# Ninth seven-product couple in the down-projections of a two-layer encoder trunk, with its weight differences formed on the fly

## The chip, the cores and the metric

The kernel runs on one core of one Trainium2 chip. The metric is the device time of one launch in microseconds (us), taken as the median of several runs. Each profile is of one execution.

The engines are called as the profile calls them: PE (TensorE; PEld is its weight load), DVE (VectorE), ACT (ScalarE), POOL (GpSimd) and SP (SyncE, which here issues nearly all DMAs).

## The reference

The trunk has two layers, 256 tokens, a model width of 2048 and an inner width of 5504, all in float32. Each layer is RMSNorm, token mixer, residual add, RMSNorm, ConvGLU, residual add. Layer 0's mixer is a bidirectional mLSTM, layer 1's a bidirectional HGRN2. The change concerns the last product of the ConvGLU, `@ w_down`:

```python
def conv_glu(hn, w_up, conv_w, conv_b, w_down):
    u = hn @ w_up
    a, v = jnp.split(u, 2, axis=-1)
    ...
    for j in range(CONV_W):
        c = c + ap[:, j:j + s] * conv_w[j]
    return (jax.nn.gelu(c, approximate=False) * v) @ w_down

    ...
    for layer in range(DEPTH):
        ...
        h = h + mix
        h = h + conv_glu(rmsnorm(h, norm_ffn_g[layer]), ...)
    return rmsnorm(h, final_g)
```

## The kernel before

**Split products.** Each float32 operand is held as a high and a low part (`wh`, `wl` for weights), and a product is three matmuls: high by high, high by low, low by high. ACT makes `wh` from a loaded weight block by a cast (line 146), DVE makes `wl` by a subtraction (line 147). Such a pair of tiles, 128x1024 or 128x512, is called a piece. Pieces are fetched three ahead of their use, and there are four `wh`/`wl` buffers, with two more in the output stages for every third piece.

**Stages.** Everything is one stream of chunks: layer 0's mixer projections and its output product, the 43 up-projection chunks (called "fm" in the code) in two halves of 22 and 21, and after each half a down-projection of that half's 22 or 21 row blocks of `w_down`. Layer 1 has the same, with its own mixer.

**Down-projection and couples.** A down-projection runs as two pairs of column blocks, one after the other: output columns 0 to 1023, then 1024 to 2047. Within a pair, two row blocks of weights make a couple, numbered `u` from 0. An ordinary couple takes eight 128x512 products, 24 matmuls. A couple listed in `SEVEN` uses Strassen's scheme of seven products, 21 matmuls; it needs sums of the activations (`sx`, made once for each half by `token_sums`, lines 546 to 551) and differences of the weight blocks (T1 to T4).

**Where the weight differences come from.** In the ConvGLU they are all formed earlier: `prepare` (line 611) loads a couple's weights while other stages run, forms the differences on DVE and stores them to DRAM (`tscr`). The down-projection then loads 1536 columns of the weights, 512 of the differences into the same `raw` tile and 1536 into a `T` tile. The mLSTM's output product does it otherwise: its three seven-product couples have nothing stored, and `combine` (lines 201 to 207) forms the differences from the couple's 2048 loaded columns by four DVE subtractions just before they are split ("on the fly").

**End of the seven-product part.** After the last listed couple of a pair, `mid` (lines 563 to 571) adds the four accumulators P1, P5, P6, P7 to the residual `hm`: one ACT copy, six DVE operations and two POOL additions. `done` (line 577) adds the other four at the pair's end. At the end of layer 0's second half the next norm's transposes (line 423) and its `xt` operands (lines 368 and 369) for the first eight row blocks are made between `mid` and the pair's end.

**Order.** A scheduler orders each engine's instructions at build time. The weight loads marked `late` keep their program order on SP's queue.

**Constants.** One tile `cst` of 928 columns, kept for the whole program, holds the identity (128 columns), two masks and a summing matrix of the mLSTM (640) and level masks of the HGRN2 (160).

The lists before are `SEVEN = (2, 3, 4, 5, 6, 7, 8, 9), (1, 2, 3, 4, 5, 6, 7)` for the first and second half, for both layers alike.

Of the kernel before, what the change touches and what calls it, by code (L numbers as in the profile page):

```python
# [8 lines left out]
F32 = mybir.dt.float32  # L9
F32R = mybir.dt.float32r  # L10
I32 = mybir.dt.int32
# [4 lines left out]
P = 128  # L16
# [30 lines left out]
LEAD = 48  # L47
TEMP = 3
GATES = 4 * AH
SEVEN = (2, 3, 4, 5, 6, 7, 8, 9), (1, 2, 3, 4, 5, 6, 7)  # L50
FIRST = 6
SPLIT = (0, 2, 5), (0, 2, 5)
END = 3
# [5 lines left out]
LEVELS = (1, 2, 4, 8, 16, 32, 64)  # L59
FINE = 5  # L60
C_ID, C_MF, C_MB, C_SUM, C_LV = 0, 128, 384, 640, 768
NCST = C_LV + FINE * QUAD


def trunk_kernel(ctx, tc, xT, x_d, fg_d, pp_d, cst_d, w_gate, w_first, w_aq, w_ak, w_av, w_ao, w_aout, w_ao2,
# [8 lines left out]
    psa = ctx.enter_context(tc.tile_pool(name="psa", bufs=4, space=PSUM))  # L74

    pp = keep.tile([P, NPP], F32, name="pp")
    cst = keep.tile([P, NCST], F32, name="cst")
    ones = keep.tile([P, T], F32, name="ones")
    pad = keep.tile([P, 8], F32, name="pad")
    hmx = keep.tile([P, 2], F32, name="mhalf")  # L80
    hm = keep.tile([P, 2, D], F32, name="hm")
    ident = cst[:, C_ID:C_ID + P]

    def col(name, i):
        o = OFF[name] + i
# [297 lines left out]
    def late(dst, src):  # L383
        tc.keep_in_program_order(nc.sync.dma_start(dst, src))
# [283 lines left out]
    def mlstm(norm, nxt):  # L668
        YT = [None] * KT
        H = 64  # L670
        stack, startup = ExitStack(), ExitStack()
        sp = startup.enter_context(tc.tile_pool(name="sp", bufs=1))
        gx = sp.tile([P, KT + KT * T], F32, name="gx")
        wg = sp.tile([P, KT * GATES], F32, name="wg")
# [4 lines left out]
        def load(loaded, follower):  # L679

            raws = [keep.tile([P, 512], F32, tag=f"yt{k}", name=f"raw{k}") for k in range(KT)]

            def w(k):
                pin(nc.sync.dma_start(raws[k], w_first[:, k * 512:(k + 1) * 512]))

            def x(q, a, b):
                q.dma_start(gx[:, a:b], xT[:, a:b])

            x(nc.scalar, 0, KT + T)
            x(nc.scalar, KT + T, KT + 2 * T)  # L690
# [12 lines left out]
            for c in range(2):  # L703
                for t in range(2):
                    late(hm[:, t, c * 1024:(c + 1) * 1024], x_d[t, :, c * 1024:(c + 1) * 1024])
            late(cst[:, 0:C_LV], cst_d[:, 0:C_LV])
            late(pp, pp_d)
            return raws

# [15 lines left out]
        def gates(gs):  # L725
            with tc.tile_pool(name="gt", bufs=1) as gp:
                R = norm.R
                gz = gp.tile([P, T], F32, name="gz")
                pg = aux("pg")
                pe.matmul(pg[:, 0:T], cst[:, C_SUM:C_SUM + P], gs, start=True, stop=True)  # L730
                dve.tensor_tensor(gz, pg[:, 0:T], R, ALU.mult)
                dve.tensor_scalar(gz, gz, col("b_gate", 0), None, ALU.add)
                xf = gp.tile([H, T], F32, tag="xf", name="xf")
                e = gp.tile([H, T], F32, name="e")
                u = gp.tile([H, T], F32, tag="u", name="u")
                l = gp.tile([H, T], F32, tag="l", name="l")
                lf = gp.tile([H, T], F32, name="lf")
                dve.tensor_scalar(xf, gz[H:P], 0.0, None, ALU.min)
                act.activation(e, gz[H:P], AF.Abs)
                act.activation(e, e, AF.Exp, scale=-1.0)  # L740
                dve.tensor_scalar(u, e, 1.0, None, ALU.add)
                act.activation(l, u, AF.Ln)
# [33 lines left out]
        segs = [  # L776
            (0, 256, 0, 0, 0, cst[:, C_MF:C_MF + 256]),
            (256, 384, 1, 0, 128, cst[:, C_MF:C_MF + 128]),
            (384, 512, 0, 1, 0, cst[:, C_MB + 128:C_MB + 256]),
            (512, 768, 1, 1, 0, cst[:, C_MB:C_MB + 256]),  # L780
        ]

        def two_parts(ps, name, scale=None):
# [162 lines left out]
    def hgrn(norm, nxt):  # L946
# [3 lines left out]

        def begin():
            mp = box["mp"] = stack.enter_context(tc.tile_pool(name="hg", bufs=1))
            late(cst[:, C_LV:], cst_d[:, C_LV:])
            prepare_early(mp, 1, 30.0, 38.0)
            box["turn"] = 0
            lb = box["lb"] = mp.tile([P, KT], F32, name="lb")
# [49 lines left out]
        def head(hd):  # L1006
# [28 lines left out]
            def both(ps):  # L1035
                return ps.rearrange("p (a b) -> p a b", a=2)

            step = SPREAD if hd < BH - 2 else STEP
            mask = [cst[:, C_LV + i * QUAD:C_LV + (i + 1) * QUAD].bitcast(I32).unsqueeze(1).broadcast_to([P, 2, QUAD])
                    for i in range(FINE)]  # L1040
            ms, n = [gather(1)], T
            yield step
# [107 lines left out]
    def ffn(layer, norm, nxt):  # L1150
# [40 lines left out]
        for part, (f0, nf) in enumerate(((0, FA), (FA, FB))):  # L1191
# [8 lines left out]
                                  todo, 18.0, (nf * 10.4 - 26.0) / len(todo), finished, late, True))  # L1200

            for i in range(nf):
                chunks.append(Chunk("fm", w_up[layer, f0 + i], KT, norm.x, done_up(f0 + i, i, GT, SX, SEVEN[part]),
                                    prep if i == 0 else None,
                                    swap=(2,) if part and i == 0 else (3,) if f0 + i == 1 else (), paced=True))
            def two(src, c0, norm, seven, shares, GT=GT, SX=SX, nf=nf):
                ch = pair(src, nf, c0, lambda k: GT[k], lambda u: SX[u], norm, seven)
                ch.waits, left = [], list(seven)
                for n, (todo, finished) in zip(shares, [early[layer]] + lists):
                    for u in left[:n]:  # L1210
                        store(ch, src, u, todo)
# [5 lines left out]
                return ch  # L1217

            w0, w1 = w_d0[layer][:, f0 * 1024:(f0 + nf) * 1024], w_d3[layer] if part else w_d1[layer]
            n = len(SEVEN[part])  # L1220
            chunks.append(two(w0, 0, nxt if part else None, SEVEN[part], (0, 0, n) if part else (FIRST, n - FIRST)))
            chunks.append(two(w1, 2, nxt if part and not ending else None, SEVEN[part], SPLIT[layer] if part else (0, n)))
            if part:
                chunks[-1].last = ending
                if ending:
# [106 lines left out]
def build(nc, ins, out_shape=(2, P, D), **kw):  # L1332
# [1 line left out]
          for k, a in ins.items()}  # L1334
    out = nc.dram_tensor("out", out_shape, F32, kind="ExternalOutput").ap()
    mscr = nc.dram_tensor("mscr", (64, T), F32, kind="Internal").ap()
    tscr = nc.dram_tensor("tscr", (len(SEVEN_MIX) + 4 * len(SEVEN[0]) + 4 * len(SEVEN[1]), P, 2048), F32, kind="Internal").ap()
    with tile.TileContext(nc, schedule_with_timeline_sim=True) as tc:  # L1338
        with ExitStack() as ctx:
            trunk_kernel(ctx, tc, ap["xT"], ap["x"], ap["fg"], ap["pp"], ap["cst"], ap["w_gate"], ap["w_first"],  # L1340
# [15 lines left out]
```

## Time and profile before

| | us |
|---|---|
| median of 3 runs | 2373.69 (2372.8 to 2375.37) |
| the profiled execution | 2372.06 |
| its span, first to last instruction | 2370.1 |
| PE busy | 2357.5 (99%) |
| DVE busy | 1965.9 (83%) |
| ACT busy | 1464.1 (62%) |
| POOL busy | 196.9 (8%) |

The granted TensorE clock is 0.999 over the span. In the profile's rows a matmul's duration is longer than its distance to the next one, since matmuls are pipelined; so the busy time of PE says that it never waits long, and what a matmul costs is read from the distance between starts. A row of the groups reads: line, engine, operation, output and inputs, shapes and count, then busy us and mean ns of one, then the idle time before them and what ended it. A row of the timeline reads: start and duration in us, engine, line, operation, names, count, and in brackets the idle time before it.

The stages that the change touches lie, in us from the span's start, at 635 to 744 (layer 0, first half), 977 to 1084 (layer 0, second half) and 1914 to 2024 (layer 1, first half). Layer 1's second half, 2256 to 2361, keeps its couples.

### The profile page before, as it was taken

The page shows a single profiled execution, that of the slowest core. Times are in us where ns is not written, and L with a number is a line of the kernel's source. Part 1 is how long each engine was busy: PE and PEld are TensorE (multiplying, and loading weights), DVE is VectorE, ACT ScalarE, POOL GpSimd, SP SyncE. Part 2 cuts the span into 40 slices and gives each one's busy share as a digit, 9 for nine tenths or more (in the row PEclk, how much of TensorE's full clock was granted, in tenths as well). Part 3 has the DMA queues.
Part 4 walks back from the last instruction along what each step waited for, and adds up shares of the span by engine and source line. Part 5 has one row for each costly group of instructions (what it writes and reads, how often), then busy time and mean ns, then how long its engine had stood idle before and what let it go on. Part 6 is the DMA issues. An engine that isn't in the chain of part 4 may idle for free. (4 is left out here: it accounts for less than half of the span.)

```text
span 2370.1 us, 38326 instructions
## 1 busy us (share of the span) xinstructions
PE 2357.5 (99%) x14548; PEld 2019.1 (85%) x14548; DVE 1965.9 (83%) x3028; ACT 1464.1 (62%) x2321; POOL 196.9 (8%) x244
## 2 busy tenths in 40 slices
PE   9999999999999999999999999999999999999998
PEld 8888888888888888888888888888888888888886
DVE  7777687888888898887887888778789888888988
ACT  7655456555565555675777777776555566555565
POOL 0100000000000000000232322220000000000000
PEclk9999999999999999999999999999999999999999
DMA  8776656888988888986666666646788898888896
GB/s 302 237 245 244 214 194 208 295 286 292 317 316 321 308 282 294 351 309 223 211 204 213 218 217 210 207 171 232 265 301 281 293 337 317 288 295 296 318 347 219
DMA packets 121832, 632.96 MB, mean 267 GB/s; under 512 B 13728, under 2 KB 14240, under 8 KB 77232
## 3 DMA queue, kind: packets, MB, share of 16 engines
q1 hardware_dynamic: 119952, 626.51, 75.0%
q0 software_dynamic: 1120, 3.21, 0.8%
q8 instruction: 114, 1.87, 0.3%
q10 hardware_dynamic: 576, 0.79, 0.1%
q14 instruction: 70, 0.57, 0.1%
HBM read 562.24 MB, written 68.22 MB: 266 GB/s over the span
## 5 line engine op out<-in xcount | busy, mean ns | idle before, releaser
L346 PE MATMUL mm<-xt,wh 128*128 128x512 f32 x3776 | 1311.6, 394 | 1.5 <-issue 1.5
L147 DVE TENSOR_TENSOR wl<-raw,wh 128x1024 fp32r<-128x1024 f32 (+1 forms) x844 | 1036.5, 1232 | 247.6 <-ACT wh L146 239.6
L146 ACT CAST wh<-raw 128x1024 fp32r<-128x1024 f32 (+1 forms) x844 | 876.1, 1043 | 528.8 <-PE mm L346 311.3
L350 PE MATMUL mm<-xt,wl 128*128 128x256 f32 x3776 | 1043.0, 278 | 0.0
L346 PEld LDWEIGHTS mm<-xt,wh 128*128 128x128 f32 x3776 | 705.5, 188 | 161.6 <-issue 1.8
L350 PEld LDWEIGHTS mm<-xt,wl 128*128 128x128 f32 x3776 | 709.2, 188 | 5.1 <-issue 0.4
L362 PE MATMUL mm<-wh,xt 128*128 128x512 f32 x1024 | 322.5, 393 | 0.8 <-ACT xt L368 0.6
L234 PE MATMUL pc<-wh,g 128*128 128x512 f32 x776 | 261.9, 390 | 0.0
L362 PEld LDWEIGHTS mm<-wh,xt 128*128 128x128 f32 x1024 | 191.5, 188 | 40.2 <-ACT xt L368 1.1
L611 DVE TENSOR_TENSOR praw<-praw 128x512 f32<-128x512 f32 x252 | 174.8, 694 | 43.7 <-DMA praw<-in_w_d 26.0
L362 PE MATMUL mm<-wl,xt 128*128 128x512 f32 x512 | 198.2, 391 | 0.0
L234 PEld LDWEIGHTS pc<-wh,g 128*128 128x128 f32 x776 | 145.6, 188 | 30.5 <-ACT wh L146 0.2
L234 PE MATMUL pc<-wl,g 128*128 128x512 f32 x388 | 151.0, 389 | 0.0
L234 PE MATMUL mm<-wh,sx 128*128 128x512 f32 x396 | 140.4, 389 | 0.0
L147 DVE TENSOR_TENSOR wl<-T,wh 128x1024 fp32r<-128x1024 f32 (+1 forms) x132 | 126.5, 969 | 12.3 <-ACT wh L146 12.1
L146 ACT CAST wh<-T 128x1024 fp32r<-128x1024 f32 (+1 forms) x132 | 109.6, 836 | 35.9 <-PE mm L234 13.1
L570 POOL TENSOR_TENSOR hm<-hm,u 128x512 f32<-128x512 f32 x10 | 14.8, 1482 | 1221.5 <-DVE u L569 1121.3
L362 PEld LDWEIGHTS mm<-wl,xt 128*128 128x128 f32 x512 | 96.2, 188 | 18.8
L1046 DVE TENSOR_TENSOR QK<-QK,G 128x256 f32<-128x256 f32 x224 | 104.7, 516 | 6.1 <-ACT kq L1025 5.7
L1170 ACT COPY avc<-mm 128x256 f32<-128x256 f32 x172 | 63.9, 372 | 65.8 <-PE mm L350 65.5
L1025 ACT COPY kq<-QK 128x512 f32<-128x512 f32 x112 | 74.5, 669 | 35.7 <-DVE QK L1046 27.8
L234 PEld LDWEIGHTS mm<-wh,sx 128*128 128x128 f32 x396 | 74.3, 188 | 15.4
(237 smaller groups left out, 2218.4 us busy)
## 6 DMA issues: line engine op xcount, KB each, us to landing
raw<-in_w_up SPq DMA_DIRECT2D x172, 1024.0 KB, 6.2
tscr<-praw SPq DMA_DIRECT2D x126, 512.0 KB, 6.7
praw<-in_w_d SPq DMA_DIRECT2D x120, 512.0 KB, 7.1
raw<-in_w_bq SPq DMA_DIRECT2D x48, 1024.0 KB, 5.0
T<-tscr SPq DMA_DIRECT2D x63, 768.0 KB, 8.1
raw<-in_w_d SPq DMA_DIRECT2D x60, 768.0 KB, 6.7
raw<-in_w_ao SPq DMA_DIRECT2D x24, 1024.0 KB, 4.8
raw<-in_w_d SPq DMA_DIRECT2D x24, 1024.0 KB, 7.4
```

Of the source, the lines that this page charges most:

```text
L146: pin(act.copy(wh[:, :m], r))
L147: pin(dve.tensor_tensor(wl[:, :m], r, wh[:, :m].bitcast(F32), ALU.subtract))
L234: pin(pe.matmul(ps, a, b, start=id(ps) not in begun, stop=stop and i == 2))
L346: pe.matmul(ps[f], wh[:, c:c + P], x, start=k + kk == 0, stop=False)
L350: pe.matmul(ps[f][:, 0:T], wl[:, c:c + P], x[:, 0:T], start=False, stop=k + kk == ch.nk - 1)
L362: pe.matmul(ps[t], x[:, a + t * P:a + (t + 1) * P], w[:, c], start=st and i == 0, stop=sp and i == 2)
L570: pool.tensor_tensor(part(1, 0), part(1, 0), u, ALU.add)
L611: dve.tensor_tensor(out, x, y, ALU.subtract)
L1025: act.copy(m, blocks(QK, h))
L1046: dve.tensor_tensor(two[:, j], two[:, j], by[:, j], ALU.mult)
L1170: act.copy(z, p[:, T:2 * T])
```

## The change

It puts one more couple on seven products in three of the four down-projections: couple 1 in the first halves of both layers (now nine), couple 8 in the second half of layer 0 (now eight). As many couples as before have stored differences. One couple of each of those halves, named in `FLY`, is formed on the fly in both pairs: couple 2 in the first halves, couple 5 in layer 0's second half. The stored ones are then couple 1 in place of 2, and couple 8 in place of 5.

The room for the ninth `sx` tile comes from `cst`: only the identity stays for the whole program, the mLSTM's masks go into a pool that is closed with the mLSTM, the HGRN2's level masks into its own pool.

```diff
-SEVEN = (2, 3, 4, 5, 6, 7, 8, 9), (1, 2, 3, 4, 5, 6, 7)
+SEVEN = ((1, 2, 3, 4, 5, 6, 7, 8, 9), (1, 2, 3, 4, 5, 6, 7, 8)), ((1, 2, 3, 4, 5, 6, 7, 8, 9), (1, 2, 3, 4, 5, 6, 7))
+FLY = (2,), (5,), (2,), ()
...
-    cst = keep.tile([P, NCST], F32, name="cst")
+    ident = keep.tile([P, P], F32, name="ident")
...
+        masks = stack.enter_context(tc.tile_pool(name="mk", bufs=1)).tile([P, MASKS], F32, name="masks")
...
-            late(cst[:, 0:C_LV], cst_d[:, 0:C_LV])
+            late(ident, cst_d[:, C_ID:C_ID + P])
+            late(masks, cst_d[:, C_MF:C_LV])
...
-            late(cst[:, C_LV:], cst_d[:, C_LV:])
+            box["lv"] = mp.tile([P, FINE * QUAD], F32, name="lv")
+            late(box["lv"], cst_d[:, C_LV:])
...
-            def two(src, c0, norm, seven, shares, GT=GT, SX=SX, nf=nf):
+            def two(src, c0, norm, seven, fly, shares, GT=GT, SX=SX, nf=nf):
                 ch = pair(src, nf, c0, lambda k: GT[k], lambda u: SX[u], norm, seven)
-                ch.waits, left = [], list(seven)
+                ch.waits, left = [], [u for u in seven if u not in fly]
...
+            seven, fly = SEVEN[layer][part], FLY[2 * layer + part]
+            n = len(seven) - len(fly)
```

The order changes on PE, DVE, ACT and SP in those three down-projections. On PE and DVE it also changes in the first products of the HGRN2's output, because every third piece takes an extra buffer and the count of pieces has shifted. Elsewhere it stays.

Place one: DVE where the first pair of layer 0's first half ends and the second begins. `u` and `hm<-hm,mm` belong to `mid`, `hm<-hm,pc` to `done`, `wl<-T` is the split of weight differences. Before:

```order
L569 TENSOR_TENSOR u<-u,mm 128x512
L577 TENSOR_TENSOR hm<-hm,pc 128x512
L147 TENSOR_TENSOR wl<-raw,wh 128x1024
L147 TENSOR_TENSOR wl<-T,wh 128x1024
L577 TENSOR_TENSOR hm<-hm,pc 128x512
L147 TENSOR_TENSOR wl<-raw,wh 128x1024
L577 TENSOR_TENSOR hm<-hm,pc 128x512
L147 TENSOR_TENSOR wl<-raw,wh 128x1024 x2
L147 TENSOR_TENSOR wl<-T,wh 128x512
L147 TENSOR_TENSOR wl<-T,wh 128x1024
```

With the change (a line number is one or more higher), the same place:

```order
L578 TENSOR_TENSOR hm<-hm,pc 128x512
L148 TENSOR_TENSOR wl<-T,wh 128x1024
L148 TENSOR_TENSOR wl<-raw,wh 128x1024
L578 TENSOR_TENSOR hm<-hm,pc 128x512
L148 TENSOR_TENSOR wl<-raw,wh 128x1024
L148 TENSOR_TENSOR wl<-T,wh 128x512
L578 TENSOR_TENSOR hm<-hm,pc 128x512
L207 TENSOR_TENSOR T<-raw 128x512
L148 TENSOR_TENSOR wl<-raw,wh 128x1024
L207 TENSOR_TENSOR raw<-raw 128x512
L207 TENSOR_TENSOR T<-raw 128x512
L207 TENSOR_TENSOR T<-raw,T 128x512
```

The four subtractions of couple 2 (line 207) now stand behind the last `hm` additions of the pair before, with one split among them.

Place two: DVE at the end of layer 0's second half, where the HGRN2's first `xt` operands are made. Before:

```order
L567 TENSOR_TENSOR hm<-hm,u 128x512
L369 TENSOR_SCALAR xt_10310<-pz,pp,xt_10310 128x256
L569 TENSOR_TENSOR u<-u,mm 128x512
L147 TENSOR_TENSOR wl<-raw,wh 128x1024
L369 TENSOR_SCALAR xt_10313<-pz,pp,xt_10313 128x256
L147 TENSOR_TENSOR wl<-raw,wh 128x1024
L369 TENSOR_SCALAR xt_10321<-pz,pp,xt_10321 128x256
L369 TENSOR_SCALAR xt_10338<-pz,pp,xt_10338 128x256
```

With the change:

```order
L568 TENSOR_TENSOR hm<-hm,u 128x512
L148 TENSOR_TENSOR wl<-raw,wh 128x1024
L570 TENSOR_TENSOR u<-u,mm 128x512
L370 TENSOR_SCALAR xt_10408<-pz,pp,xt_10408 128x256
L370 TENSOR_SCALAR xt_10419<-pz,pp,xt_10419 128x256
L148 TENSOR_TENSOR wl<-raw,wh 128x1024
L370 TENSOR_SCALAR xt_10436<-pz,pp,xt_10436 128x256
L578 TENSOR_TENSOR hm<-hm,pc 128x512
L370 TENSOR_SCALAR xt_10411<-pz,pp,xt_10411 128x256
L370 TENSOR_SCALAR xt_10422<-pz,pp,xt_10422 128x256
```

The `xt` writes now stand later, among the pair's last `hm<-hm,pc` additions, because `mid` follows couple 8 instead of couple 7 and only one ordinary couple and the odd row block are left behind it.

More of the change, by code (lines that the diff above doesn't have):

```diff
@@ L61 @@
 C_ID, C_MF, C_MB, C_SUM, C_LV = 0, 128, 384, 640, 768
+MASKS = C_LV - C_MF
 NCST = C_LV + FINE * QUAD
@@ L81, in trunk_kernel @@
     hm = keep.tile([P, 2, D], F32, name="hm")
-    ident = cst[:, C_ID:C_ID + P]
     def col(name, i):
@@ L671, in mlstm @@
         stack, startup = ExitStack(), ExitStack()
+        masks = stack.enter_context(tc.tile_pool(name="mk", bufs=1)).tile([P, MASKS], F32, name="masks")
+        MF, MB, SUM = (masks[:, o - C_MF:o - C_MF + n] for o, n in ((C_MF, 256), (C_MB, 256), (C_SUM, 128)))
         sp = startup.enter_context(tc.tile_pool(name="sp", bufs=1))
@@ L729, in gates @@
                 pg = aux("pg")
-                pe.matmul(pg[:, 0:T], cst[:, C_SUM:C_SUM + P], gs, start=True, stop=True)
+                pe.matmul(pg[:, 0:T], SUM, gs, start=True, stop=True)
                 dve.tensor_tensor(gz, pg[:, 0:T], R, ALU.mult)
@@ L776, in mlstm @@
         segs = [
[L777 to L780, printed above, removed]
+            (0, 256, 0, 0, 0, MF),
+            (256, 384, 1, 0, 128, MF[:, 0:128]),
+            (384, 512, 0, 1, 0, MB[:, 128:256]),
+            (512, 768, 1, 1, 0, MB),
         ]
@@ L1038, in head @@
             step = SPREAD if hd < BH - 2 else STEP
-            mask = [cst[:, C_LV + i * QUAD:C_LV + (i + 1) * QUAD].bitcast(I32).unsqueeze(1).broadcast_to([P, 2, QUAD])
+            mask = [box["lv"][:, i * QUAD:(i + 1) * QUAD].bitcast(I32).unsqueeze(1).broadcast_to([P, 2, QUAD])
                     for i in range(FINE)]
@@ L1202, in ffn @@
             for i in range(nf):
-                chunks.append(Chunk("fm", w_up[layer, f0 + i], KT, norm.x, done_up(f0 + i, i, GT, SX, SEVEN[part]),
+                chunks.append(Chunk("fm", w_up[layer, f0 + i], KT, norm.x, done_up(f0 + i, i, GT, SX, SEVEN[layer][part]),
                                     prep if i == 0 else None,
                                     swap=(2,) if part and i == 0 else (3,) if f0 + i == 1 else (), paced=True))
-            def two(src, c0, norm, seven, shares, GT=GT, SX=SX, nf=nf):
+            def two(src, c0, norm, seven, fly, shares, GT=GT, SX=SX, nf=nf):
                 ch = pair(src, nf, c0, lambda k: GT[k], lambda u: SX[u], norm, seven)
-                ch.waits, left = [], list(seven)
+                ch.waits, left = [], [u for u in seven if u not in fly]
                 for n, (todo, finished) in zip(shares, [early[layer]] + lists):
@@ L1219, in ffn @@
             w0, w1 = w_d0[layer][:, f0 * 1024:(f0 + nf) * 1024], w_d3[layer] if part else w_d1[layer]
-            n = len(SEVEN[part])
-            chunks.append(two(w0, 0, nxt if part else None, SEVEN[part], (0, 0, n) if part else (FIRST, n - FIRST)))
-            chunks.append(two(w1, 2, nxt if part and not ending else None, SEVEN[part], SPLIT[layer] if part else (0, n)))
+            seven, fly = SEVEN[layer][part], FLY[2 * layer + part]
+            n = len(seven) - len(fly)
+            chunks.append(two(w0, 0, nxt if part else None, seven, fly, (0, 0, n) if part else (FIRST, n - FIRST)))
+            chunks.append(two(w1, 2, nxt if part and not ending else None, seven, fly, SPLIT[layer] if part else (0, n)))
             if part:
@@ L1336, in build @@
     mscr = nc.dram_tensor("mscr", (64, T), F32, kind="Internal").ap()
-    tscr = nc.dram_tensor("tscr", (len(SEVEN_MIX) + 4 * len(SEVEN[0]) + 4 * len(SEVEN[1]), P, 2048), F32, kind="Internal").ap()
+    tscr = nc.dram_tensor("tscr", (len(SEVEN_MIX) + 2 * sum(len(s) for layer in SEVEN for s in layer), P, 2048), F32, kind="Internal").ap()
     with tile.TileContext(nc, schedule_with_timeline_sim=True) as tc:
```

## The prediction

> **What bounds the kernel now.** I read the page's engine lines first, then who PE waits for, then the down-projections by windows.
>
> ```profile
> PE 2357.5 (99%) x14548; PEld 2019.1 (85%) x14548; DVE 1965.9 (83%) x3028; ACT 1464.1 (62%) x2321; POOL 196.9 (8%) x244
> ```
>
> The waits of PE, whole:
>
> ```profile
> PE mm L346 <- issue: 1.5, 1, 1.5
> PE idle L1239 <- POOL ones L1232: 1.1, 1, 1.1
> PE mm L362 <- ACT xt L368: 0.6, 1, 0.6
> PE pc L234 <- DVE wl L147: 0.4, 1, 0.4
> ```
>
> PE waits 3.6 us in the whole program, and never in a ConvGLU. Time can be gained there only by giving PE less to do, and lost only where another engine becomes late. By windows (columns: length, then busy us of PE, PEld, DVE, ACT and POOL with their counts, granted clock, DMA share, GB/s), the three down-projections that change, then the mLSTM's output product, then a stretch inside a run of listed couples:
>
> ```profile
> 635.30:744.60 109.30, 109.30 (x485) 90.52 (x484) 93.34 (x101) 71.16 (x82) 4.06 (x3) 1.00 0.87 323
> 977.10:1083.80 106.70, 106.70 (x481) 88.40 (x480) 92.60 (x103) 73.69 (x94) 8.00 (x4) 1.00 0.84 308
> 1914.50:2023.80 109.30, 109.30 (x484) 90.53 (x483) 94.50 (x103) 71.69 (x84) 4.00 (x3) 1.00 0.88 325
> 324.00:365.00 41.00, 41.00 (x183) 33.95 (x182) 35.73 (x43) 23.42 (x29) 0.00 (x0) 1.00 0.57 193
> 650.00:680.00 30.00, 30.00 (x134) 24.82 (x133) 25.56 (x26) 22.88 (x25) 0.00 (x0) 1.00 1.00 379
> ```
>
> PE is busy for the whole of each, at a clock of 1.00. DVE is idle for 16.0, 14.1 and 14.8 us of the first three, and only after that comes ACT.
>
> **What a removed matmul is worth.** The group's row shows 390 ns, but DVE's timeline in a run of listed couples shows what paces it:
>
> ```profile
> L234 PE MATMUL pc<-wh,g 128*128 128x512 f32 x776 | 261.9, 390 | 0.0
> ```
>
> ```profile
> 656.53 1.23 DVE L147 TENSOR_TENSOR wl<-raw,wh 128x1024 fp32r<-128x1024 f32 x1 [0.66 <-ACT wh L146]
> 657.68 1.22 DVE L147 TENSOR_TENSOR wl<-T,wh 128x1024 fp32r<-128x1024 f32 x1
> 658.81 1.22 DVE L147 TENSOR_TENSOR wl<-raw,wh 128x1024 fp32r<-128x1024 f32 x1
> 659.95 0.69 DVE L147 TENSOR_TENSOR wl<-T,wh 128x512 fp32r<-128x512 f32 x1
> 661.29 1.23 DVE L147 TENSOR_TENSOR wl<-raw,wh 128x1024 fp32r<-128x1024 f32 x1 [0.66 <-ACT wh L146]
> ```
>
> One couple passes from 656.53 to 661.29, in 4.76 us, and each time DVE waits 0.66 us until a buffer that PE has left is refilled. So PE sets the pace: 4.76 us for 21 matmuls, 0.2267 us each. An ordinary couple, with 24, takes 5.44 us, 0.68 more. The change makes couples of this kind out of three, each in two pairs: 6 x 0.68 = **4.08 us**, 18 matmuls. By the order of PE's instructions 18 are indeed gone, and nothing is added there, so that the change doesn't do this is ruled out.
>
> The Trainium skill, "TensorE: Matmul & The Clock Gate", section "Back-to-back issue gap", has about 131 ns a matmul in a sustained stream with 512 columns; the gain would then be 18 x 0.131 = 2.4 us, as an estimate. The distance measured here is 0.2267 us, and I keep to that.
>
> **What it adds, and what covers it.** Splits of differences and the subtractions on the fly, priced by rows of the mLSTM's output, which does the same already:
>
> ```profile
> 328.03 0.68 DVE L206 TENSOR_TENSOR T<-raw,T 128x512 f32<-128x512 f32 x1
> 328.63 1.23 DVE L147 TENSOR_TENSOR wl<-T,wh 128x1024 fp32r<-128x1024 f32 x1
> ```
>
> From start to start a 512-column operation takes 0.60 us on DVE, a 1024-column one 1.13 to 1.15 (the rows at 657.68 and 658.81). Each added couple needs in each pair a split of 1024 and one of 512 (1.13 + 0.60), and a couple on the fly four subtractions (2.40): 4.13 us, 24.8 us for all six, 8.3 in each down-projection. Each down-projection gets 1.4 us shorter. Of DVE's 16.0, 14.1 and 14.8 us of idle time 6.3, 4.4 and 5.1 are left. ACT gets two casts more:
>
> ```profile
> L146 ACT CAST wh<-T 128x1024 fp32r<-128x1024 f32 x66 | 69.3, 1050 | 20.4 <-DMA T<-tscr 7.5 <-DMA raw<-in_w_d 4.5 <-PE pc L234 3.2
> L146 ACT CAST wh<-T 128x512 fp32r<-128x512 f32 x66 | 41.0, 621 | 15.5 <-PE mm L234 10.9 <-PE pc L234 4.0
> ```
>
> That is at most 3.3 us a down-projection, of 33 or more us idle: nothing. The token sums of three more couples lie on DVE in the up-projections:
>
> ```profile
> L546 DVE TENSOR_TENSOR avc<-avc 128x128 f32<-128x128 f32 x120 | 34.9, 291 | 3.5
> L548 DVE TENSOR_TENSOR sx<-avc,sx 128x384 fp32r<-128x384 f32 x30 | 16.6, 552 | 0.0
> ```
>
> Four of 0.29, one of 0.55 and a shorter one make 2 us a half, once in some 230 us: nothing; uncovered they would cost 6.
>
> So on the sum DVE has room; what matters is where the subtractions stand. A stored couple leaves DVE 0.66 us, an ordinary one 5.44 - 2 x 1.14 = 3.2, one on the fly takes 2.40 - 0.66 = 1.7 more than PE gives. The cover is DVE's lead: the split at 656.53 ends at 657.76, its first matmul is this one, 3.6 us later:
>
> ```profile
> 661.37 0.39 PE L234 MATMUL mm<-wl,g 128*128 128x512 f32 x1
> ```
>
> **Inside a run** (couple 5 of layer 0's second half, couple 2 of each first pair) the lead falls from 3.6 to 1.9 and grows again by 0.66 a couple: nothing lost. For couple 1 a `T` tile must now be there earlier:
>
> ```profile
> 622.74 2.60 SPq L614 DMA_DIRECT2D tscr<-praw  x2
> ```
>
> ```profile
> T<-tscr SPq DMA_DIRECT2D x63, 768.0 KB, 8.1
> ```
>
> Its load stands behind these stores on SP's queue: issued at about 626, landed at about 634, cast by 635, and in the new order its first matmul is the 32nd of the down-projection, 7 us after 635.3. Covered by some 5 us. DMA moves the same bytes in each half, but the run of stored couples, in which its share is 1.00, is cut from eight to seven behind one that needs only its weights.
>
> **Between two pairs** the lead is shortest. Before, in layer 0's first half:
>
> ```profile
> 690.21 0.68 DVE L577 TENSOR_TENSOR hm<-hm,pc 128x512 f32<-128x512 f32 x1
> 690.80 2.04 DVE L147 TENSOR_TENSOR wl<-raw,wh 128x1024 fp32r<-128x1024 f32 x1
> 692.77 2.31 DVE L147 TENSOR_TENSOR wl<-T,wh 128x1024 fp32r<-128x1024 f32 x1
> ```
>
> ```profile
> 690.46 1.30 POOL L570 TENSOR_TENSOR hm<-hm,u 128x512 f32<-128x512 f32 x1 [296.65 <-DVE u L569]
> 691.71 2.29 POOL L571 TENSOR_TENSOR hm<-hm,u 128x512 f32<-128x512 f32 x1
> ```
>
> ```profile
> 693.55 0.39 PE L234 MATMUL pc<-wl,g 128*128 128x512 f32 x1
> 696.05 0.39 PE L234 MATMUL mm<-wl,sx 128*128 128x512 f32 x1
> ```
>
> The two splits end at 692.84 and 695.08, 0.7 and 1.0 us before these, their first matmuls; beside POOL's two additions they take 2.04 and 2.31 us instead of 1.22. Around this place three ordinary couples stood in a row and restored the lead; now there are two, the third is a couple with differences, and the one formed on the fly comes right behind it. But the new order puts `mid`'s work ahead of the splits, so that POOL starts earlier. I lay that order out from the last P1 product, with 0.60 and 1.13 us for each row, 1.0 more for a split beside POOL, and 0.2267 us a matmul: the split after POOL starts is done at 8.3 for a matmul at 9.3, the split behind the last subtraction at 19.4 for one at 20.2. An estimate, and it leaves 0.8 to 1.0 us, no more than before. What waits behind the subtractions on DVE is those splits, and PE waits for them.
>
> The Trainium skill, "SBUF — State Buffer", section "Who interferes with whom", says that a DVE instruction with two SBUF inputs contends with a GpSimd instruction that reads SBUF. The two slow splits agree. The subtractions have two SBUF inputs as well; by that rule any that fell beside POOL's additions would nearly double, which the order avoids by two splits and three additions.
>
> **At the end of layer 0** `mid` now follows couple 8, so the list up to the next norm's `xt` has one ordinary couple, 5.4 us, less room. Its cover:
>
> ```profile
> 1075.07 1.40 DVE L147 TENSOR_TENSOR wl<-raw,wh 128x1024 fp32r<-128x1024 f32 x1 [1.06 <-ACT wh L146]
> ```
>
> ```profile
> 1083.91 0.39 PE L362 MATMUL mm<-wl,xt 128*128 128x512 f32 x1
> ```
>
> The HGRN2's first split is 7.4 us early, so 2.0 are left. Laid out like the other place, the fourth `xt` comes 0.6 us before its matmul.
>
> **The rest.** The HGRN2's output is ordered anew at one place, where PE waited once:
>
> ```profile
> 1610.53 0.50 PE L234 MATMUL pc<-wl,yb 128*128 128x512 f32 x1 [0.36 <-DVE wl L147]
> ```
>
> The split it waited for now stands seven short operations earlier: between a gain of 0.4 and a loss of 0.4, taken as 0. The constants come by one DMA more at the start, tens of us ahead of their use: 0. `lv` keeps its place between the HGRN2's first loads; its room was a `T` tile's, whose last reader, a split of couple 8 at the latest, stands ahead of the loads before it: 0, and uncovered one landing:
>
> ```profile
> cst<-in_cst SPq DMA_DIRECT2D x1, 80.0 KB, 5.6
> ```
>
> **The sum.** 4.08 us gained. Losses: 0 if the two layouts hold; where a split's lead was gone, at 1610.53, it cost about 0.4. I take that for two of the four tight places: 0.8. The profiled execution would go from 2372.06 (span 2370.1) to 2368.8; it lies 1.6 below the median of the runs, so the median goes from 2373.69 to **2370.4 us**, -0.14%. About 0.2%, 4.7 us, is what a measurement of this kernel can tell from no change; the gain in full is below that.
>
> **The rivals.**
> - *A gain in full and more (0.13).* The leads hold, and the waits of 1.5 and 0.4 us on PE outside the ConvGLUs go too, since the program's layout has moved: 2373.7 - 4.1 - 1.9 = 2367.7. For: they are single events. Against: nothing in the change touches the larger.
> - *A matmul is worth its busy time (0.05).* 18 x 0.390 = 7.0: 2366.7. Against: the couples' pace.
> - *The gain is eaten (0.16).* At the three boundaries and the end of layer 0 DVE comes 1 us late: 2373.7. For: leads of 0.6 to 1.0 in my layouts.
> - *Slower: DVE no longer covers the subtractions (0.10).* All 24 stand in PE's way: 24 x 0.60 = 14.4, less 4.1: 2384.0. It decides itself at the couple on the fly: from the point where DVE arrives there with under 1.7 us of lead, the rest is PE's wait, and a late `raw` or `T` load (DMA share 1.00 in the run) would bring that about. Against: the mLSTM's output forms three of eight couples on the fly with PE at 41.00 of 41.00 us; but ordinary couples lie between them.
> - *My forecast* has the rest, 0.56.
>
> The range is 2367.5 to 2375.2: from the first rival to the third with a run's scatter (1.5 us here), leaving out the second, the fourth and the tails. Faster by over 0.2%: the first two and a tail of the forecast, 0.2; slower: the fourth and a tail, 0.12; the rest, 0.68.
>
> **What would show it.** Right: 18 matmuls fewer on L235 (before L234), couples still at 4.76 us, the three down-projections at about 107.9, 105.3 and 107.9 us, DVE about 101 us busy in each, waits of PE for `wl` of at most 1 us in all. Wrong: PE waiting for DVE or ACT behind L207 (the subtractions) in a second pair, a gap of PE at the start of the HGRN2 that ends with an `xt`, or a couple on the fly that takes over 4.76 us.

## The result and the profile after

| | before | after |
|---|---|---|
| median of 7 runs each, same chip | 2372.8 (2371.69 to 2375.37) | 2379.44 (2378.54 to 2382.02) |
| span of the profiled execution | 2370.1 | 2377.5 |

The ratio is 1.0029, 95% interval [1.0019, 1.0038]: 0.28% slower, where 0.14% faster was forecast. The time lies above the forecast's range, and the interval leaves out a ratio of 1.

The engine line of the page after, and the waits of PE, whole:

```profile
PE 2365.9 (100%) x14530; PEld 2021.9 (85%) x14530; DVE 1995.3 (84%) x3082; ACT 1470.6 (62%) x2339; POOL 194.6 (8%) x244
```

```profile
PE mm L363 <- ACT xt L369: 1.5, 1, 1.5
PE idle L1245 <- POOL ones L1238: 1.1, 1, 1.1
```

PE has 18 instructions fewer, waits 2.6 us instead of 3.6, and is busy 8.4 us longer. So the loss is no wait for DVE, ACT or a load: PE takes longer for work that it never stops doing. The view by windows says where. First the three down-projections that the change touches, after (before they took 109.28, 106.62 and 109.28; the prediction shows them some hundredths apart), then the HGRN2's output product after and before:

```profile
639.55:747.40 107.85, 107.80 (x476) 88.89 (x475) 99.84 (x112) 72.85 (x87) 3.53 (x2) 1.00 0.85 320
980.36:1086.17 105.81, 105.66 (x475) 87.28 (x473) 98.50 (x112) 74.66 (x97) 7.01 (x4) 1.00 0.80 295
1919.07:2027.03 107.96, 107.96 (x479) 89.34 (x478) 100.36 (x112) 73.75 (x86) 4.01 (x3) 1.00 0.86 322
1601.48:1644.57 43.09, 43.09 (x192) 35.63 (x191) 35.97 (x53) 24.29 (x31) 0.00 (x0) 1.00 0.67 244
1600.60:1644.44 43.84, 43.48 (x193) 35.48 (x191) 36.20 (x53) 24.53 (x32) 0.00 (x0) 1.00 0.69 240
```

The down-projections came out nearly as laid out: 107.9, 105.8 and 108.0 us against 107.9, 105.3 and 107.9, with DVE busy 98.5 to 100.4 us in each. Now the four up-projections, each from its first matmul behind the stage ahead to the first of its down-projection, before:

```profile
389.71:635.27 245.56, 245.56 (x1421) 214.76 (x1420) 211.31 (x343) 140.72 (x221) 0.70 (x1) 1.00 0.84 292
744.55:977.06 232.51, 232.51 (x1344) 203.28 (x1342) 201.46 (x316) 128.76 (x200) 3.08 (x2) 1.00 0.87 303
1668.97:1914.54 245.57, 245.57 (x1422) 214.84 (x1420) 210.83 (x341) 139.76 (x219) 0.70 (x1) 1.00 0.84 292
2023.82:2256.32 232.50, 232.50 (x1343) 203.36 (x1342) 200.04 (x316) 128.89 (x199) 5.29 (x6) 1.00 0.86 303
```

and after:

```profile
389.62:639.55 249.93, 249.93 (x1421) 216.89 (x1420) 213.77 (x349) 141.06 (x223) 0.70 (x1) 1.00 0.84 290
747.40:980.36 232.96, 232.96 (x1346) 203.65 (x1345) 204.24 (x324) 128.94 (x201) 3.54 (x2) 1.00 0.86 301
1669.14:1919.07 249.93, 249.93 (x1422) 216.90 (x1420) 214.88 (x350) 140.23 (x223) 0.70 (x1) 1.00 0.83 290
2027.03:2263.89 236.86, 236.86 (x1343) 205.49 (x1342) 202.14 (x316) 127.28 (x199) 5.29 (x6) 1.00 0.86 296
```

Three of the four take 4.36 to 4.37 us more with the same number of matmuls at the same clock of 1.00, 13.1 together. The second takes 0.45 more only because two of its matmuls now stand inside it instead of in the down-projection ahead, which is shorter by as much. The last one's half was not touched by the change at all.

What a slower stage looks like is seen in PE's timeline. Each step is a pair: 512 columns on `wh` (L346, after L347), 256 on `wl` (L350, after L351). Before, in layer 0's first half:

```profile
500.07 0.39 PE L346 MATMUL mm<-xt,wh 128*128 128x512 f32 x1
500.31 0.27 PE L350 MATMUL mm<-xt,wl 128*128 128x256 f32 x1
500.42 0.40 PE L346 MATMUL mm<-xt,wh 128*128 128x512 f32 x1
500.65 0.28 PE L350 MATMUL mm<-xt,wl 128*128 128x256 f32 x1
500.77 0.39 PE L346 MATMUL mm<-xt,wh 128*128 128x512 f32 x1
```

The trace holds the starts to the nanosecond: distances of 230, 113, 232 and 118 ns, over and over, two pairs in 693 ns, 346.7 a pair over the stage. After, in the same stage:

```profile
500.69 0.40 PE L347 MATMUL mm<-xt,wh 128*128 128x512 f32 x1
500.93 0.28 PE L351 MATMUL mm<-xt,wl 128*128 128x256 f32 x1
501.05 0.40 PE L347 MATMUL mm<-xt,wh 128*128 128x512 f32 x1
501.29 0.28 PE L351 MATMUL mm<-xt,wl 128*128 128x256 f32 x1
501.40 0.40 PE L347 MATMUL mm<-xt,wh 128*128 128x512 f32 x1
501.63 0.28 PE L351 MATMUL mm<-xt,wl 128*128 128x256 f32 x1
501.75 0.40 PE L347 MATMUL mm<-xt,wh 128*128 128x512 f32 x1
```

Here it is 241, 120, 235, 114, 232, 118: three pairs in 1060 ns, 353.3 a pair, and again without end. I call them the **short** and the **long** pattern (the expectations below say fast and slow). A whole stage runs in one of them: taken 32 pairs at a time, the mean is 346.7 all through the one kind of stage and 353.1 to 353.5 all through the other, but for the first chunk or two.

The start of the long pattern in layer 1's second half can be seen:

```profile
2031.65 0.28 PE L351 MATMUL mm<-xt,wl 128*128 128x256 f32 x1
2031.77 0.39 PE L347 MATMUL mm<-xt,wh 128*128 128x512 f32 x1
2032.00 0.27 PE L351 MATMUL mm<-xt,wl 128*128 128x256 f32 x1
2032.12 0.62 PE L347 MATMUL mm<-xt,wh 128*128 128x512 f32 x2
2032.58 0.40 PE L351 MATMUL mm<-xt,wl 128*128 128x256 f32 x2
2032.81 0.40 PE L347 MATMUL mm<-xt,wh 128*128 128x512 f32 x1
2033.04 0.28 PE L351 MATMUL mm<-xt,wl 128*128 128x256 f32 x1
2033.16 0.40 PE L347 MATMUL mm<-xt,wh 128*128 128x512 f32 x1
2033.40 0.28 PE L351 MATMUL mm<-xt,wl 128*128 128x256 f32 x1
```

At 2032.12 the ninth `xt` tile's matmuls come as high, high, low, low instead of high, low, high, low: an exchange of two neighbours. Ahead of it the pattern is short, behind it long. In the trace of before this tile has four single rows:

```profile
2028.91 0.40 PE L346 MATMUL mm<-xt,wh 128*128 128x512 f32 x1
2029.14 0.28 PE L350 MATMUL mm<-xt,wl 128*128 128x256 f32 x1
2029.26 0.39 PE L346 MATMUL mm<-xt,wh 128*128 128x512 f32 x1
2029.49 0.27 PE L350 MATMUL mm<-xt,wl 128*128 128x256 f32 x1
```

In the order of instructions of after the scheduler has made two double ones:

```
L351 MATMUL mm<-xt_17244,wl 128x256
L347 MATMUL mm<-xt_17284,wh 128x512 x2
L351 MATMUL mm<-xt_17284,wl 128x256 x2
L347 MATMUL mm<-xt_17287,wh 128x512
```

So "Elsewhere it stays", as said above of the order, is wrong here. In the first halves the order is the same in both kernels. There one exchange is written in the code (`swap=(3,)`, in the second chunk of each layer), and behind it before is in the short pattern, after in the long.

### The profile page after: what moved, and what is told of

Same layout as the page of the kernel before. It is cut to its first block, busy times and chain, and to the rows that moved or that the text cites. A ratio compares the mean times of both kernels' runs of the same rounds, so it can differ in the third digit from the quotient of the medians.

```text
span 2377.5 us, 38370 instructions
## 1 busy us (share of the span) xinstructions
PE 2365.9 (100%) x14530; PEld 2021.9 (85%) x14530; DVE 1995.3 (84%) x3082; ACT 1470.6 (62%) x2339; POOL 194.6 (8%) x244
## 5 line engine op out<-in xcount | busy, mean ns | idle before, releaser
L347 PE MATMUL mm<-xt,wh 128*128 128x512 f32 x3776 | 1324.7, 397 | 0.0
L351 PE MATMUL mm<-xt,wl 128*128 128x256 f32 x3776 | 1050.6, 280 | 0.0
L347 PEld LDWEIGHTS mm<-xt,wh 128*128 128x128 f32 x3776 | 706.2, 188 | 166.8
L351 PEld LDWEIGHTS mm<-xt,wl 128*128 128x128 f32 x3776 | 711.6, 188 | 5.2 <-issue 0.4
L235 PE MATMUL pc<-wh,g 128*128 128x512 f32 x716 | 244.3, 389 | 0.1
L235 PEld LDWEIGHTS pc<-wh,g 128*128 128x128 f32 x716 | 134.4, 188 | 28.5 <-ACT wh L147 0.5
L235 PE MATMUL mm<-wh,sx 128*128 128x512 f32 x432 | 153.3, 389 | 0.0
L148 DVE TENSOR_TENSOR wl<-T,wh 128x1024 fp32r<-128x1024 f32 (+1 forms) x144 | 135.9, 955 | 15.2 <-ACT wh L147 14.4
L147 ACT CAST wh<-T 128x1024 fp32r<-128x1024 f32 (+1 forms) x144 | 118.7, 835 | 47.9 <-DMA T<-tscr 18.3
L235 PE MATMUL pc<-wl,g 128*128 128x512 f32 x358 | 139.4, 389 | 0.0
L235 PEld LDWEIGHTS mm<-wh,sx 128*128 128x128 f32 x432 | 81.1, 188 | 16.8
```

Of the source, the lines that this page charges most:

```text
L147: pin(act.copy(wh[:, :m], r))
L148: pin(dve.tensor_tensor(wl[:, :m], r, wh[:, :m].bitcast(F32), ALU.subtract))
L235: pin(pe.matmul(ps, a, b, start=id(ps) not in begun, stop=stop and i == 2))
L347: pe.matmul(ps[f], wh[:, c:c + P], x, start=k + kk == 0, stop=False)
L351: pe.matmul(ps[f][:, 0:T], wl[:, c:c + P], x[:, 0:T], start=False, stop=k + kk == ch.nk - 1)
```

## The experiments

Theory A: the loss is only these patterns; which one PE settles in follows from the state in which it comes to a disturbance, an exchange above all. Theory B: the added couples' work slows the up-projections. The table has the lengths of the four up-projections (us) from windows like those above (233.0 is 232.5 and the two matmuls that stand inside it), and the median of the runs; before, run along with each group of four, had 2372.88, 2372.37 and 2372.70.

| | L0 first | L0 second | L1 first | L1 second | median |
|---|---|---|---|---|---|
| before | 245.6 | 232.5 | 245.6 | 232.5 | 2372.8 |
| after | 249.9 | 233.0 | 249.9 | 236.9 | 2379.4 |
| e1_memory | 249.9 | 232.5 | 249.9 | 232.5 | 2380.5 |
| e2_noswap | 245.5 | 233.0 | 245.5 | 236.9 | 2371.1 |
| e3_pin | 249.9 | 233.0 | 249.9 | 232.5 | 2378.3 |
| e4_force | 245.6 | 232.5 | 245.6 | 236.9 | 2376.6 |
| e5_both | 245.5 | 233.0 | 245.5 | 232.5 | 2368.6 |
| e6_before_noswap | 250.0 | 232.5 | 250.0 | 232.5 | 2381.1 |
| e7_room | 245.6 | 232.5 | 245.6 | 232.5 | 2371.3 |
| e8_room_hm | 249.9 | 232.5 | 249.9 | 232.5 | 2379.7 |
| e9_toggle | 245.5 | 233.0 | 249.9 | 236.9 | 2375.5 |
| e10_place | 245.5 | 233.0 | 249.9 | 236.9 | 2376.9 |
| e11_room32 | 250.0 | 233.0 | 250.0 | 236.9 | 2380.6 |
| e12_seven | 245.5 | 233.0 | 245.5 | 233.0 | 2370.0 |

**The memory move alone** (the kernel after with the old lists):

```diff
-SEVEN = ((1, 2, 3, 4, 5, 6, 7, 8, 9), (1, 2, 3, 4, 5, 6, 7, 8)), ((1, 2, 3, 4, 5, 6, 7, 8, 9), (1, 2, 3, 4, 5, 6, 7))
-FLY = (2,), (5,), (2,), ()
+SEVEN = ((2, 3, 4, 5, 6, 7, 8, 9), (1, 2, 3, 4, 5, 6, 7)), ((2, 3, 4, 5, 6, 7, 8, 9), (1, 2, 3, 4, 5, 6, 7))
+FLY = (), (), (), ()
```

> The kernel after with the lists of before: only the constants are split and moved (masks into the mLSTM's pool, lv into the HGRN2's), so every tile behind them lies 3200 bytes lower; TensorE's order is that of before. Theory A (TensorE falls into one of two repeating patterns, 346.7 or 353.3 ns a pair of matmuls, and what it falls into is fixed by the state in which it enters; the addresses or the transposes' own tile change that state): both first halves' up-projections at 353.3 ns a pair, the second halves at 346.7, time about 8.5 us over before, 2381. Theory B (the added couples' own work, sums on DVE or loads, slows the up-projections): 346.7 in all four, time as before, 2373.

2380.49, ratio 1.0034 [1.0021, 1.0048]. Its first up-projection:

```profile
389.72:639.65 249.93, 249.93 (x1421) 216.90 (x1420) 211.98 (x343) 140.44 (x221) 0.70 (x1) 1.00 0.84 287
```

The whole loss of the first halves is there without one added couple. Theory B falls for them.

**No exchange of place 3** (in after, then in before):

```diff
-                                    swap=(2,) if part and i == 0 else (3,) if f0 + i == 1 else (), paced=True))
+                                    swap=(2,) if part and i == 0 else (), paced=True))
```

> The kernel after without the one exchange of two neighbouring matmuls in the second up-projection chunk of each layer (swap of place 3); the two rows in each layer are all that changes in TensorE's order. Theory A: the exchange is the place at which the pattern of 353.3 ns a pair began in the first halves; without it they go on as they enter, at 347, and the time falls by about 8.5 us, to 2371; the second half of layer 1 stays at 353. Theory B: no change, 2379.4, and 353 in both first halves.

> The kernel before without the exchange of place 3. Theory A: before enters that chunk in the slow pattern (241, 120, 236, 113, 233, 117 ns) and the exchange is what ends it there; without it both first halves go on at 353.3 ns a pair, 8.4 us more, 2381. The same edit that takes 8.3 us from after. Rival (the exchange itself is harmful wherever it stands): as before or faster, 2372 or less.

In after: 2371.13, ratio to before 0.9993 [0.9983, 1.0002]. In before: 2381.13, ratio 1.0040 [1.0024, 1.0055]. The first up-projection of the one and of the other:

```profile
389.44:634.93 245.49, 245.49 (x1421) 214.67 (x1420) 213.26 (x349) 141.33 (x223) 0.70 (x1) 1.00 0.85 294
```

```profile
389.50:639.52 250.02, 250.02 (x1422) 217.10 (x1420) 212.02 (x343) 140.52 (x221) 0.70 (x1) 1.00 0.84 288
```

The same edit takes 8.3 us from the one kernel and gives 8.8 to the other. Before comes to this chunk in the long pattern, and the exchange ends it (231, 112, 233, 117 ns behind it); after comes in a third one (230 and 117 ns, 347 a pair), and the exchange starts the long (241, 120, 236, 113, 232, 118).

**The exchange in layer 1's second half**, taken out of after and put into before (`pin` holds written order):

```diff
+                        fix = pin if k + kk == ch.hold else lambda ins: ins
...
-                            pe.matmul(ps[f], wh[:, c:c + P], x, start=k + kk == 0, stop=False)
+                            fix(pe.matmul(ps[f], wh[:, c:c + P], x, start=k + kk == 0, stop=False))
...
+                                    hold=8 if layer and part and i == 0 else None))
```

and for before, besides:

```diff
+                    if ch.hold and k == ch.hold:
+                        ops[1:3] = ops[2], ops[1]
```

> The kernel after with the four matmuls of the ninth xt tile in the first chunk of layer 1's second half held in written order (high, low, high, low); that is the one exchange by which TensorE's order of after differs there from before. Theory A: this half goes at 346.7 ns a pair from its start to its end, 4.3 us less, time 2375; the first halves stay at 353. Theory B: no change, 2379.4.

> The kernel before with that one exchange put in (high, high, low, low on the ninth xt tile in the first chunk of layer 1's second half), nothing else. Theory A: this half falls into 353.3 ns a pair from there on and the program takes about 4.3 us more than before, 2377; all other halves as before. Theory B: as before, 2373.

e3: 2378.29, ratio to before 1.0023 [1.0014, 1.0033]. e4: 2376.59, ratio 1.0020 [1.0010, 1.0029]. Layer 1's second up-projection in e3, then its last down-projection, then the up-projection in e4:

```profile
2027.11:2259.61 232.50, 232.50 (x1343) 203.35 (x1342) 201.57 (x316) 127.42 (x198) 5.28 (x6) 1.00 0.86 302
```

```profile
2259.61:2365.58 105.97, 105.44 (x464) 86.30 (x462) 90.44 (x107) 69.32 (x89) 7.72 (x5) 1.00 0.78 291
```

```profile
2023.26:2260.13 236.87, 236.87 (x1344) 205.49 (x1342) 203.41 (x318) 129.70 (x202) 5.30 (x6) 1.00 0.86 299
```

One exchange among 14,530 matmuls moves the stage by 4.37 us, both ways. In time e3 gained less than that: its profiled execution took 3.2 us less than that of after, since 1.06 came back in the last down-projection (105.97 against 104.91), and its median fell by 1.2 only, within a scatter of 6 us over its runs. The stage is shown, the 4.3 us of program time for e3 are not.

**Both edits, the couples kept.**

> The kernel after without the exchange of place 3 in both layers' second chunk, and with the ninth xt tile's matmuls of layer 1's second half in written order: both edits together, all couples of the change kept. Theory A (the loss is the pattern of matmul distances alone): all four up-projections at 346.7 to 346.8 ns a pair, and 8.3 and 4.4 us less than after: 2366.8, some 6 under before, made of the 18 matmuls' 4.1 and of waits of 1.5 to 2 that are gone. Theory C (a part of the loss belongs to the couples and has been hidden by the patterns): the patterns at 346.7 and the time not under 2370.

2368.59, ratio to before 0.9987 [0.9978, 0.9995]: faster than both kernels. All four stages are short. The median lies 1.8 above the expectation, the profiled execution 0.8. In the latter, layer 0's second down-projection takes 107.34 instead of the 105.81 of after (first row). About 0.9 of this 1.5 lies at the boundary between its two pairs, 0.5 in longer distances between matmuls 21 to 24 us after its start. The wait at the boundary is in the second row, what DVE did there in the third:

```profile
975.62:1082.96 107.34, 106.50 (x475) 86.99 (x474) 99.69 (x113) 74.84 (x97) 6.11 (x4) 1.00 0.79 292
```

```profile
1028.73 0.47 PE L235 MATMUL pc<-wh,g 128*128 128x512 f32 x1 [0.69 <-DVE hm L579]
```

```profile
1023.61 4.38 DVE L148 TENSOR_TENSOR wl<-raw,wh 128x1024 fp32r<-128x1024 f32 x2 [0.33 <-ACT wh L147]
```

At the boundary two splits run beside POOL's additions, at 2.2 us each, and `done` comes late behind them. This is a small case of the rival in which the gain is eaten at the tight places. In after's profiled execution the same two splits took 3.46, and PE waited for nothing there.

**What sets the state of entry.** In the kernel of the memory move alone (e1), an unused tile of 800 columns is put behind `ident` (e7), so that all tiles behind it lie again where they lie in before, or behind `hm` (e8), so that only those behind `hm` do. In after, one of 32 columns ahead of `hm` (e11) raises `hm` and all behind it by 128 bytes. The edit of e7:

```diff
     ident = keep.tile([P, P], F32, name="ident")
+    room = keep.tile([P, 800], F32, name="room")
...
+    pool.memset(room, 0.0)
```

> The kernel of the memory move alone (lists of before) with an unused tile of 800 columns behind ident, so that all tiles behind lie again where they lie in before; only the masks, lv and their loads differ. If the addresses set the state in which TensorE enters (theory A1): all four halves at 346.7 to 346.9, 2373. If ident as a tile of its own, or the loads, set it (A2): both first halves stay at 353.2, 2380.5.

> The same unused tile behind hm: ones, hm stay 3200 bytes lower, xt, raw, wh and wl lie as in before. If the addresses of the transposes' operand hm set the state: both first halves at 353.2, 2380.5. If those of xt, wh and wl: 346.9, 2373.

> The kernel after with an unused tile of 32 columns ahead of hm: hm and all behind it 128 bytes higher, at 7872, which has the same remainder by 256 (192) as before's 10944, where after's 7744 has 64. If that remainder of hm's address sets the state in which TensorE leaves the transposes: both first halves enter as in before, and the exchange ends the slow pattern: 346.9 ns a pair, 2371. If it is another property of the address: 353.2, 2379.4, or another pattern.

e7: 2371.34, ratio 0.9997 [0.9987, 1.0007]; e8: 2379.74, 1.0033 [1.0020, 1.0046]; e11: 2380.60, 1.0034 [1.0024, 1.0045]. The first up-projection of each:

```profile
389.40:634.97 245.57, 245.57 (x1422) 214.79 (x1420) 211.48 (x343) 140.59 (x221) 0.70 (x1) 1.00 0.85 292
```

```profile
388.40:638.32 249.92, 249.92 (x1421) 217.02 (x1420) 212.40 (x343) 140.43 (x221) 0.70 (x1) 1.00 0.84 288
```

```profile
389.27:639.28 250.01, 250.01 (x1421) 216.99 (x1420) 214.60 (x350) 141.13 (x223) 0.70 (x1) 1.00 0.84 290
```

The addresses decide, not the split of the constants: e7 differs from e1 in nothing else but the tile's one write at the start. Of the tiles that lie differently in e7 and e8 (`ones`, two small ones, `hm`) PE reads two in this stage, both in its first chunk: `hm` in eight transposes, and `ones` in four matmuls 3 us behind the last of them. The distances differ ahead of those four already: behind the last transpose they are 203, 229, 117, 234, 117, 241 ns with `hm` at its old place (e7), and 205, 233, 124, 229, 117, 230 at the new one (e1; e8 within 2 ns). The rule that I tried in e11, the address's remainder by 256, is half a miss: the entry was the long pattern again, as in before, but the exchange met it at another point of its period and did not end it. But e11 does not decide against the remainder: up to the four matmuls on `ones` its distances are those of before to 1 ns, and behind them they are not (199, 236, 113, 233 against 202, 231, 117, 241), and `ones` lies 3200 bytes lower in e11 than in before. Which property of the address counts, and whether that of `ones` does too, is open.

**Is an exchange a switch?** A second exchange in after, at place 9 (e9, layer 0), 10 (e9, layer 1) and 11 (e10, layer 0), and the one exchange at place 4 (e10, layer 1):

```diff
-                                    swap=(2,) if part and i == 0 else (3,) if f0 + i == 1 else (), paced=True))
+                                    swap=(2,) if part and i == 0 else ((3, 9), (3, 10))[layer] if f0 + i == 1 else (), paced=True))
```

> The kernel after with a second exchange of two matmuls in the second chunk of each first half, behind the one of place 3: at place 9 in layer 0, at place 10 in layer 1. Theory T (an exchange ends a repeating pattern and the stream settles anew; in the runs so far one exchange always led from the fast pattern to the slow one or back): from place 9 and 10 on both halves go at 346.7 ns a pair, time as without the exchange of place 3, 2371. Rival P (what follows depends on where in the pattern's period of three pairs the exchange falls): at least one of the two layers stays at 353.2; with one of them 2375, with both 2379.4.

> The kernel after with two further variants: layer 0 has a second exchange at place 11 (the third position in the slow pattern's period), layer 1 has its one exchange at place 4 instead of 3 (the other position in the period of two pairs). Theory T: layer 0 at 346.7 ns from there on, layer 1 at 353.2, since one exchange toggles wherever it stands: 2375. Rival P: layer 0 may stay at 353.2 and layer 1 may stay at 346.7.

e9: 2375.48, ratio 1.0012 [1.0001, 1.0022]; e10: 2376.88, 1.0020 [1.0010, 1.0030]. e9's first up-projections in layers 0 and 1:

```profile
391.38:636.91 245.53, 245.53 (x1421) 214.85 (x1420) 213.46 (x349) 141.55 (x223) 0.70 (x1) 1.00 0.85 294
1666.02:1915.95 249.93, 249.93 (x1422) 217.10 (x1421) 214.67 (x350) 140.35 (x223) 0.70 (x1) 1.00 0.84 289
```

At 9 and 11 the long pattern ended, at 10 it went on; ahead of these places the distances of the two layers agree within a nanosecond. At place 4 the long one began, as at place 3, so that e10 came out in both layers as theory T said; its median lies 1.9 over T's 2375, and its runs are up to 7 us apart. The one case against T is place 10: there the exchange did not end the pattern. So an exchange is no switch that toggles wherever it stands. That the position in the period of three pairs decides fits the three places, each of which was run once.

**Couple 8 and the one on the fly left out of e5** (`FLY = (2,), (), (2,), ()`, seven couples in layer 0's second half):

> The kernel with both edits (no exchange of place 3, the ninth xt tile in written order) and the old list of seven couples in layer 0's second half; nine couples stay in both first halves. If couple 8 and the one on the fly bring their 1.36 us there: 1.4 us over the version with both edits, 2370. If they cost what they bring, by the waits of 1.5 us at layer 0's second boundary between two pairs (loads that land late): as that version, 2368.6, and no wait there.

2370.01, ratio 0.9989 [0.9980, 0.9998]. Its profiled span is 2365.1, that of e5 2365.6; the medians stand the other way, 1.4 apart, and the intervals overlap. Whether the change pays in this half is undecided. The traces don't show that it does. Layer 0's second down-projection took 105.4 to 107.3 us in the seven profiled executions in which it has eight couples (after, e2, e3, e5, e9, e10, e11), and 106.6 in each of the seven in which it has seven; e12's, against the 107.34 of e5:

```profile
974.68:1081.27 106.59, 106.59 (x480) 88.35 (x479) 90.95 (x104) 73.33 (x96) 7.03 (x4) 1.00 0.80 292
```

## Why the prediction was wrong

**What held.**

- *18 matmuls at 0.2267 us:* the down-projection of layer 1's first half, which has lost its six and nothing else, fell by 1.32 us (109.28 to 107.96), 0.22 a matmul. Layer 0's fell by 1.43; 0.45 of that are the two matmuls that moved into the next stage, so the couples brought 1.0. The Trainium skill, "TensorE: Matmul & The Clock Gate", section "Back-to-back issue gap", gives about 131 ns a matmul for 512 columns in a sustained stream; six would then have been worth 0.8 us, as an estimate, and the trace decides against it.
- *DVE and its cover:* DVE was busy within 3 us of the 101 forecast, and no wait of PE for `wl` is left.
- *The stray wait of 1.5 us* on PE is gone from the trace of after, as in the rival with "a gain in full and more": that HGRN2 stretch took 48.1 us instead of 49.7. But it stands in the trace of e4 and not in those of e6, e7 and e8, all of which have the order of before there, so no run shows that the change removed it.
- *The tight places:* 0.8 us was taken for four of them, and they cost about 0.9: 0.33 at the boundary between the pairs of layer 0's first half, and 0.55 in layer 0's second, which gained 0.81 of its 1.36 (at its end five transposes now stand bare ahead of the HGRN2's first product, the row below). That this sum came out is partly luck, since the second of these stages took up to 1.5 us more in other executions with the same couples. The HGRN2's output, taken as 0, gained 0.75: its wait for a split is in the trace of before and not in that of after.

```profile
1085.10 1.00 PE L424 MATMUL pz<-ident,hm 128*128 128x128 f32 x5
```

**What failed.** The step that failed stands in this sentence on PE in the ConvGLU: "Time can be gained there only by giving PE less to do, and lost only where another engine becomes late." PE lost 13.1 us there while no other engine was late. So the sum has terms for the down-projections alone, and takes for granted that stages whose work and order stay the same keep their time: the text ahead says "Elsewhere it stays", and the prediction counts the constants' move only by its load, "The constants come by one DMA more at the start, tens of us ahead of their use: 0." The missing term is 4.37 + 4.36 + 4.36 = 13.1 us. With it the ledger of the two profiled executions closes: 1.0 (layer 0's first half) + 1.3 (layer 1's) + 0.8 (layer 0's second) + 0.75 (the HGRN2's output) + 1.65 (the stray wait's stretch) = 5.5 gained, 13.1 lost, 7.6 net; the spans differ by 7.4. Two causes, both shown: the constants' move put `ones`, `hm` and all behind them 3200 bytes lower, so that PE came to the exchange of place 3 in another pattern (two stages, 8.7 us: e1 against e7, and e2), and the scheduler made one exchange in a half that the change does not touch (4.4 us, e3 and e4). Why PE has these patterns is not shown.

**The rivals.** None had this mechanism. Rival one did say that "the program's layout has moved", but only as a way to gain. The rival on the slow side, DVE no longer covering the subtractions, named a time 4.6 us too high and a mechanism that did not occur.

**What could have been seen.** Both patterns stand in the trace of before: its first up-projection begins in the long one and goes over to the short one at the exchange, so that its length hangs on something finer than any wait. And the one exchange stands in the order of the changed kernel.

## What to carry to other kernels

On an engine that never waits, compare the distance between starts stage by stage, and first of all in stages that the change does not touch; busy time and lists of waits hide a slower rhythm (here PE's busy share even rose from 99 to 100%). The Trainium skill says, in "Perfetto Trace Analysis", section "Identifying the Most-Contended Engine", that the busy share of matmuls is not a good measure of how close a kernel is to roofline, because pipelined instructions look smaller in the trace; this trace agrees that it is no good measure, PE's busy time rose by 8.4 us over 18 matmuls fewer. In a long run of like instructions that never waits, moving a tile or exchanging two neighbours can cost or bring more than the edit itself, as it did here (13.1 us against 4.1). So price the layout and the order of a change apart from its work, and tune them again after it.

## What the runs showed of the hardware

The same pairs of matmuls, with the same shapes at the same granted clock, run in one of two stable rhythms, 346.7 or 353.3 ns a pair (1.9% apart), for some 230 us on end, in all 14 traces. Two things decided which one: the order of two neighbouring matmuls (e2, e3, e4, e6), and, by the state in which PE comes to such a place, the address of another tile, read by eight transposes of 128 columns some 8 us earlier (e7 against e8; the distances part behind those transposes). Why these rhythms exist, and what in the address counts, stays open.
